# Seven block products in place of eight in two of the six gate/up groups of each feed-forward layer

## The chip, the cores and the metric

The program runs on one core of one Trainium2 chip. The metric is device microseconds of one execution of the whole program. The profile adds the time line of each engine: PE is the matrix engine TensorE (PEld its weight load), DVE is VectorE, ACT is ScalarE, POOL is GpSimd, SP is SyncE, which here issues nearly all transfers.

## The reference

The kernel computes a trunk of four pre-norm layers on one sequence of 256 tokens with 1024 features, all in float32. Each layer adds a token mixer (layers 0 and 3 a sparse attention with compressed, selected and windowed keys, "NSA"; layer 1 a block-sparse attention, "MoBA"; layer 2 a short gated convolution) and then a gated feed-forward network, the "FFN". A last normalisation follows.

```python
D_FF = -(-8 * D_MODEL // (3 * 256)) * 256          # 2816

def swiglu(a, w_gate, w_up, w_down):
    return (jax.nn.silu(a @ w_gate) * (a @ w_up)) @ w_down
...
        h = h + m                                   # m: the mixer's output
        a = rms_norm(h, norm_ffn[i])
        h = h + swiglu(a, ffn_w_gate[i], ffn_w_up[i], ffn_w_down[i])
    return rms_norm(h, norm_final)
```

The change is in `a @ w_gate` and `a @ w_up`: 256 tokens by 1024 features, times two matrices of 1024 by 2816.

## The kernel before

**Operands in two halves.** The matrix engine reads float32 in the type fp32r. Each operand is therefore split in two tiles, a rounded one ("hi", in code `whi`) and what is left ("lo", `wlo` = operand − hi), and a product is three matmuls: hi·hi, hi·lo, lo·hi. For weights the hi copy is made by ScalarE (L119) and the subtraction by VectorE (L123).

**The weight stream.** All weights lie in DRAM as one stream of blocks of 128 × 128, in the order of use. Eight blocks are a *part*: 128 × 1024 elements, 512 KB. `take` hands out the next blocks. When a part is first taken, the parts up to `AHEAD` = 5 (itself included) are loaded and split (`load_part`, `split_part`); there are 4 raw buffers and `W_BUFS` = 5 buffers each of hi and lo. So the two splitting engines may run about four parts ahead of the matrix engine and no further.

**An FFN layer.** `ffn` first computes the gate and up products in groups of up to four column tiles of 128: g = 0, 4, 8, 12, 16 have four, the last, g = 20, has two. In a group of four, two halves of the tokens times gate and up give four accumulators of 128 tokens × 512 columns in PSUM (one bank each; a layer has banks of three tags, A with 4, B with 3, C with 1). Each of the 8 feature tiles k takes 8 blocks, one part: 4 of gate, 4 of up. The matmuls have 128 tokens of the activations as their stationary operand and 512 weight columns as the moving one. A part is 12 matmuls (2 token halves × gate/up × 3), a group of four is 96:

```python
w = [self.take(4) for _ in outs[0]]
for t in range(NT):
    s = slice(t * P, (t + 1) * P)
    for o, (hi, lo) in zip(outs[t], w):
        mm(o, a[:, 0, s], hi, start=(k == 0), stop=False)
        mm(o, a[:, 0, s], lo, start=False, stop=False)
        mm(o, a[:, 1, s], hi, start=False, stop=(k == KT - 1))
```

**Closing a group.** `hidden` applies, for each token half, silu(rstd · gate) on ScalarE (L304), the product with rstd · up on VectorE (L305) and a transposition in 32 × 32 squares on VectorE (L306). The squares are put in place by 16 transfers of SP (`move`, L316, tiles `pt`), four for each part that follows. Two parts after the last of them, `split` makes the hi and lo tiles `ff` of the result (four copies on ScalarE at L202, four subtractions on VectorE at L203). `take` runs these jobs when the stream reaches their part. The down projection (`out_proj`, or `finish` in the last layer) needs `ff` later.

**The norm.** `rstd` = (mean of squares)^−½ of each token is not known when group 0 starts: products are made with the unscaled activations and scaled at the closing. `square` collects the sum of squares `ssq` (ScalarE and GpSimd), the matrix engine sums it over features (`rms_sums`, during the last tile of group 0), and `rms_tokens` computes `rstd` with VectorE (`var`) and GpSimd (L244).

**Order.** The instructions of an engine run in the order in which a scheduler of the framework puts them (by its estimate of what is ready), not as written. Banks and buffers are handed on in the order of their release.

Of the kernel before, what the change touches and what calls it, by code (L numbers as in the profile page):

```python
# [16 lines left out]
P = 128  # L17
# [42 lines left out]
class Kernel:  # L60
    def __init__(self, ctx, tc, ap):
        self.tc, self.nc, self.ap = tc, tc.nc, ap
        self.operands = ctx.enter_context(tc.tile_pool(name="operands", bufs=2))
        self.const = ctx.enter_context(tc.tile_pool(name="const", bufs=1))
        self.wp = ctx.enter_context(tc.tile_pool(name="wp", bufs=3))
        self.work = ctx.enter_context(tc.tile_pool(name="work", bufs=2))
        self.ps = ctx.enter_context(tc.tile_pool(name="ps", bufs=2, space=PSUM))
        self.pos = 0
        self.raw = {}
        self.parts = {}  # L70
        self.jobs = []
        self.nblk = ap["w"].shape[0]
        self.names = [step for step, name, _, c in stream()
                      for _ in range(len(c) // P * (FT if name == "ffn_w_down" else 4 if step == "F" else KT))][::PART]
        self.n = 0

    def uid(self, s):
# [23 lines left out]
    def split_part(self, q):  # L101
        nc = self.nc
        if self.names[q] == "F":
            t = self.operands.tile([P, PART * P], F32, tag="whi", name=f"wf{q}", bufs=W_BUFS)
            nc.sync.dma_start(t, self.ap["w"][q])
            self.parts[q] = (t, t)
            return
        if q not in self.raw:
            self.load_part(q)
        src = self.raw.pop(q)  # L110
        hi = self.operands.tile([P, PART * P], F32R, tag="whi", name=f"whi{q}", bufs=W_BUFS)
        lo = self.operands.tile([P, PART * P], F32R, tag="wlo", name=f"wlo{q}", bufs=W_BUFS)
        lo_eng, hi_eng = (e.get(self.names[q], d) for e, d in ((LO, "v"), (HI, "a")))
        eng = {"p": nc.gpsimd, "v": nc.vector}[lo_eng[q % len(lo_eng)] if q >= 4 else "v"]
        copy = {"a": nc.scalar.copy, "v": nc.vector.tensor_copy}[hi_eng[q % len(hi_eng)] if q >= 4 else "a"]
        n = PART * P // (2 if q < 4 else 1)
        for o in range(0, PART * P, n):
            c = slice(o, o + n)
            copy(hi[:, c], src[:, c])  # L119
            m = n // (PIECES if eng is nc.gpsimd else 1)  # L120
            for b in range(o, o + n, m):
                d = slice(b, b + m)
                eng.tensor_tensor(out=lo[:, d], in0=src[:, d], in1=hi[:, d].bitcast(F32), op=OP.subtract)  # L123
        self.parts[q] = (hi, lo)

    def take(self, n=1):

        q, o = divmod(self.pos, PART)
        assert o + n <= PART
        for x in range(q, min(q + AHEAD, self.nblk)):  # L130
# [156 lines left out]
    def ffn(self, norm):  # L287
# [4 lines left out]
        hs = []  # L292
        q = P // 4
        self.moved = 0

        def hidden(banks, n):

# [3 lines left out]
            for t, (pg, pu) in enumerate(banks):  # L301
                r = self.rstd[:, t:t + 1]
                sg, hf = (self.sb([P, n * P], "pr", bufs=PR_BUFS) for _ in range(2))
                nc.scalar.activation(sg, pg, AF.Silu, scale=r)  # L304
                nc.vector.scalar_tensor_tensor(hf, pu, r, sg, op0=OP.mult, op1=OP.mult)  # L305
                nc.vector.transpose(turned[:, t], hf)  # L306
            rows = self.sb([P, NT, 4, n * q], "pt", bufs=PT_BUFS)
            dst, ds = [self.ff([P, 2, S]) for _ in range(n)], []
            hs.extend(dst)
# [15 lines left out]
            part = max(self.pos // PART + 3, self.moved)  # L325
            for i in range(0, 16, MOVES):
                self.jobs.append((part, move(i)))
                part += 1
            self.moved = part
            self.jobs.append((part + 2, split))  # L330

        for g in range(0, FT, 4):
            n = min(4, FT - g)
            if n == 4:
                banks = [[self.bank(c) for c in row] for row in (("AA", "AA") if g % 8 else ("BB", "BC"))]
                outs = banks
            else:
                outs = [[self.bank("B")] for _ in range(NT)]
                banks = [(o[:, :S], o[:, S:]) for o, in outs]
# [10 lines left out]
            if self.rstd is None:  # L350
                self.rms_tokens()
            hidden(banks, n)
        (self.out_proj if norm < 7 else self.finish)(hs, norm + 1)


    def finish(self, hs, norm):
        nc = self.nc
# [102 lines left out]
    def put_keys(self, dst, p):  # L460
# [3 lines left out]
        for i in range(2):  # L464
            r = slice(i * DH, (i + 1) * DH)
            nc.scalar.copy(dst[r, 0, i, :], f[r])
            nc.vector.tensor_tensor(out=dst[r, 1, i, :], in0=f[r], in1=dst[r, 0, i, :].bitcast(F32), op=OP.subtract)

    def pad_keys(self):
# [79 lines left out]
    def nsa(self, j, norm):  # L549
        nc, at = self.nc, self.begin(norm)  # L550
        mm = nc.tensor.matmul
        w2 = self.sb([P, 2, 2, P], "w2", bufs=1)
        nc.sync.dma_start(w2, self.ap["w2"][j])
        pos = self.sb([P, 2, 16], "pos", bufs=1)
# [326 lines left out]
    def run(self):  # L881
# [39 lines left out]
        self.keys = [const.tile([P, 2, 2, S], F32R, tag=f"keys{i}", name=f"keys{i}") for i in range(4)]  # L921
# [16 lines left out]

def wide_tiles(w, cols):
# [5 lines left out]
def stream():  # L945
# [4 lines left out]
    for i in LAYERS:  # L950
# [36 lines left out]
def tiles(x):  # L987
# [56 lines left out]
```

## Time and profile before

| | |
|---|---|
| time of the kernel, median of 3 runs | 1249.42 us (1249.18 to 1249.9) |
| the profiled execution, its span | 1247.6 us |
| what the median is above the span | 1.8 us |
| busy: PE / PEld | 1225.3 / 1061.5 us |
| busy: DVE / ACT / POOL | 875.0 / 675.6 / 227.3 us |
| the four FFN layers start at | 158.8, 456.7, 729.2, 1059 us |

The span is what the profiler saw between the first and the last instruction; the run's time is counted on the device and has a little around it. "Busy" is the union of an engine's instructions; PE's instructions overlap (a matmul is listed with about 0.39 us while one starts each 0.23 us), so its share tells that work was always queued, not that it was at its fastest. Everything from 20 to 158 us is the mixer of layer 0; the others lie between the FFN layers, at 340 to 457, 638 to 729 and 910 to 1059 us.

### The profile page before, as it was taken

The numbers are of one execution on the slowest core, as the hardware profiler recorded it, in microseconds if no ns is written. First come the engines' busy times: TensorE is split into PE (matmuls) and PEld (weight loads), VectorE is DVE, ScalarE is ACT, GpSimd is POOL, SyncE is SP. The second block draws the span as 40 slices with busy tenths as digits, with TensorE's granted clock in tenths as the row PEclk, the third lists the DMA queues.
The fourth block names the chain that finished last, engine by engine and source line by source line (L and its number), as shares of the span: only waits on it lengthen the run. The fifth ranks groups of instructions, "written<-read, shape, count | busy, mean of one in ns | idle before, by whom it ended". The sixth has DMA issues, their size and how long they took to land.

```text
span 1247.6 us, 19344 instructions
## 1 busy us (share of the span) xinstructions
PE 1225.3 (98%) x6788; PEld 1061.5 (85%) x6788; DVE 875.0 (70%) x1653; ACT 675.6 (54%) x1218; POOL 227.3 (18%) x357
## 2 busy tenths in 40 slices
PE   8999999999999999999999999999999999999997
PEld 8987888888899888888888888888899878888886
DVE  7778785665778795656769886565747797756553
ACT  5588754544456544545444545454446896555443
POOL 1067600000111520000113210000220676000000
PEclk9998999999999999999999999999999999999999
DMA  8741166767555347666665666776666312676772
GB/s 288 247 126 49 52 220 198 239 198 231 188 170 153 102 140 209 216 212 208 220 196 167 195 201 195 212 236 195 208 204 210 118 38 71 208 228 213 226 224 72
DMA packets 91585, 227.20 MB, mean 182 GB/s; under 512 B 17504, under 2 KB 38368, under 8 KB 91488
## 3 DMA queue, kind: packets, MB, share of 16 engines
q1 hardware_dynamic: 91056, 225.41, 57.6%
q8 instruction: 53, 0.87, 0.3%
q10 hardware_dynamic: 432, 0.56, 0.1%
q14 instruction: 44, 0.36, 0.1%
HBM read 213.33 MB, written 1.05 MB: 172 GB/s over the span
## 4 chain that ended last, share of the span: by engine, by line
PE 87%; DVE 5%; ACT 4%; POOL 2%; issue 1%; DMA 1%; POOLq 0%; ACTq 0%; DVEq 0%
PE psA L163 13%; PE psA L167 7%; PE psB L347 6%; PE psB L349 6%; PE psB L348 6%; PE psA L348 5%; PE psA L349 5%; PE psA L347 5%; PE psA L143 2%; PE psB L640 2%; PE psA L144 2%; PE psA L145 2%; PE psB L163 2%; DVE wlo L123 2%; PE psC L349 2%; PE psC L347 2%
## 5 line engine op out<-in xcount | busy, mean ns | idle before, releaser
L123 DVE TENSOR_TENSOR wlo<-raw,whi 128x1024 fp32r<-128x1024 f32 (+1 forms) x366 | 441.0, 1215 | 261.7 <-ACT whi L119 213.7
L119 ACT CAST whi<-raw 128x1024 fp32r<-128x1024 f32 (+1 forms) x379 | 393.2, 1039 | 425.9 <-PE psC L349 91.3
L163 PE MATMUL psA<-ff,whi 128*128 128x512 f32 x686 | 181.5, 393 | 0.1
L163 PEld LDWEIGHTS psA<-ff,whi 128*128 128x128 f32 x686 | 124.6, 189 | 22.7 <-DVE row L847 0.6
L347 PE MATMUL psB<-whi,at 128*128 128x512 f32 x352 | 137.6, 391 | 0.2 <-ACT pr L304 0.2
L349 PE MATMUL psB<-whi,at 128*128 128x512 f32 x352 | 137.2, 390 | 0.0
L348 PE MATMUL psB<-wlo,at 128*128 128x512 f32 x352 | 137.1, 389 | 0.0
L230 POOL TENSOR_TENSOR ssq<-ssq,row 128x256 f32<-128x256 f32 x42 | 33.6, 799 | 393.0 <-ACT row L228 392.2
L143 PE MATMUL psA<-at,whi 128*128 128x256 f32 x352 | 101.3, 288 | 2.0 <-DVE row L411 2.0
L167 PE MATMUL psA<-ff,wlo 128*128 128x256 f32 x686 | 101.5, 283 | 0.0
L167 PEld LDWEIGHTS psA<-ff,wlo 128*128 128x128 f32 x686 | 96.2, 191 | 5.3
L145 PE MATMUL psA<-at,wlo 128*128 128x256 f32 x352 | 99.9, 284 | 0.0
L144 PE MATMUL psA<-at,whi 128*128 128x256 f32 x352 | 99.9, 284 | 0.0
L349 PE MATMUL psA<-whi,at 128*128 128x512 f32 x256 | 99.7, 389 | 0.0
L347 PE MATMUL psA<-whi,at 128*128 128x512 f32 x256 | 99.7, 389 | 0.0
L348 PE MATMUL psA<-wlo,at 128*128 128x512 f32 x256 | 99.7, 389 | 0.0
L448 POOL TENSOR_SCALAR pr<-pr,rc,gates 128x256 f32<-128x256 f32 (+1 forms) x128 | 73.7, 590 | 112.6 <-DVE rc L446 111.3
L347 PEld LDWEIGHTS psB<-whi,at 128*128 128x128 f32 x352 | 66.1, 188 | 14.0 <-ACT pr L304 0.6
L349 PEld LDWEIGHTS psB<-whi,at 128*128 128x128 f32 x352 | 66.1, 188 | 13.8
L348 PEld LDWEIGHTS psB<-wlo,at 128*128 128x128 f32 x352 | 66.1, 188 | 13.6
L123 POOL TENSOR_TENSOR wlo<-raw,whi 128x256 fp32r<-128x256 f32 x96 | 69.6, 763 | 36.7 <-ACT whi L119 16.6
L444 ACT ACTIVATE pr<-pr,mn 128x128 f32<-128x128 f32 (+1 forms) x160 | 71.2, 448 | 5.7 <-DVE mn L441 5.0
(239 smaller groups left out, 2256.1 us busy)
## 6 DMA issues: line engine op xcount, KB each, us to landing
raw<-in_w SPq DMA_DIRECT2D x384, 512.0 KB, 4.3
pt<-pt SPq DMA_DIRECT2D x320, 32.0 KB, 3.1
wf<-in_w SPq DMA_DIRECT2D x16, 512.0 KB, 4.5
h<-in_xt SPq DMA_DIRECT2D x4, 256.0 KB, 4.5
raw<-in_w SPq DMA_DIRECT2D x4, 256.0 KB, 4.8
pt<-pt SPq DMA_DIRECT2D x64, 16.0 KB, 2.9
w<-in_w SPq DMA_DIRECT2D x2, 256.0 KB, 3.9
pt<-in_gfin SPq DMA_DIRECT2D x1, 512.0 KB, 3.9
```

Source lines behind the costliest of these rows:

```text
L119: copy(hi[:, c], src[:, c])
L123: eng.tensor_tensor(out=lo[:, d], in0=src[:, d], in1=hi[:, d].bitcast(F32), op=OP.subtract)
L143: mm(out, wt[0], act[0], start=first, stop=False)
L144: mm(out, wt[0], act[1], start=False, stop=False)
L145: mm(out, wt[1], act[0], start=False, stop=last)
L163: mm(outs[o], w[0], acts[k].rearrange("p i s -> p (i s)"), start=(k == 0), stop=(k == n - 1))
L167: mm(outs[o][:, :S], w[1], acts[k][:, 0, :], start=False, stop=False)
L347: mm(o, a[:, 0, s], hi, start=(k == 0), stop=False)
L348: mm(o, a[:, 0, s], lo, start=False, stop=False)
L349: mm(o, a[:, 1, s], hi, start=False, stop=(k == KT - 1))
L444: nc.scalar.activation(pr[:, c], pr[:, c], AF.Exp, bias=mn[:, j:j + 1], scale=-1.0, accum_out=den[:, j:j + 1])
L448: getattr(nc, PR[j % len(PR)]).tensor_scalar(pr[:, c], pr[:, c], rc[:, j:j + 1], gates[j], op0=OP.mult, op1=OP.mult)
```

## The change

In groups g = 8 and g = 16 of each FFN layer, the first four feature tiles (k = 0 to 3) are computed as a 2 × 2 block matrix product with seven block products in place of eight (Strassen's scheme in Winograd's form). The blocks of the left matrix are (token half) × (k 0–1 or k 2–3), those of the right matrix are (k 0–1 or k 2–3) × (gate or up): B11 is gate and B12 up of k 0–1, B21 gate and B22 up of k 2–3, each 8 blocks in size, one part. Sums of the right blocks are made by VectorE in place: T1 = B12 − B11, T3 = B22 − B12, T2 = B22 − T1, T4 = B21 − T2. A *product* takes one such part, hi and lo, for 6 matmuls of 128 × 512 (2 feature tiles × 3). The tiles k = 4 to 7 stay as they were, 12 matmuls a part. Sums of the left blocks are made once in a layer by GpSimd (`token_sums`).

```diff
-W_BUFS = 5
+W_BUFS = 6
-FF_BUFS = 24
+FF_BUFS = 26
+FAST = ("B11", "T1", "B21", "T2", "B22", "T4", "T3")
+FAST_GROUPS = (8, 16)
+FFN_BANKS = ("BB BA", "AA AB", "BBAA", "AA BB", "BAAB", "B A")
+KX_BUFS = 4
...
+    def fast_part(self, x):
+        q, what = self.seq[x]
+        if what == "B11":
+            self.blocks = {}
+            for i, n in enumerate(("B11", "B12", "B22", "B21")):
+                t = self.blocks[n] = self.block(n)
+                self.load = self.nc.sync.dma_start(t, self.ap["w"][q + i])
+        b = self.blocks
+        hi = self.operands.tile([P, PART * P], F32R, tag="whi", name=f"shi{x}", bufs=W_BUFS)
+        lo = self.operands.tile([P, PART * P], F32R, tag="wlo", name=f"slo{x}", bufs=W_BUFS)
+        self.nc.scalar.copy(hi, b[what])
+        self.nc.vector.tensor_tensor(out=lo, in0=b[what], in1=hi.bitcast(F32), op=OP.subtract)
+        self.parts[x] = (hi, lo)
+        if what == "B11":
+            b["T1"] = self.combine(b["B11"], b["B12"], b["B11"])
+            b["T3"] = self.combine(b["B12"], b["B22"], b["B12"])
+        elif what == "T1":
+            b["T2"] = self.combine(b["T1"], b["B22"], b["T1"])
+        elif what == "B21":
+            b["T4"] = self.combine(b["B21"], b["B21"], b["T2"])
...
+        ahead = AHEAD + (self.names[self.seq[q][0]] in ("ffn", "fast"))
-        while self.jobs and self.jobs[0][0] <= q:
+        while self.jobs and self.jobs[0][0] <= self.when[q]:
...
+            up1, up0, gate0, gate1 = (self.bank(c) for c in tags)
+            product(up1, tokens(0, 0), True)
+            p1 = self.sb([P, 512], "gu")
+            copy(p1, up1, 0)
+            product(up0, summed(0), True)
+            p5 = self.sb([P, 512], "ph", bufs=1)
+            copy(p5, up0, 1)
+            product(gate0, tokens(2, 0), True)
+            product(up1, summed(1), False)
+            u2 = self.sb([P, 512], "pr", bufs=PR_BUFS)
+            copy(u2, up1, 0)
+            product(up0, summed(3), False)
+            product(gate1, tokens(2, 1), True)
+            product(up1, summed(2), False)
+            u3 = self.sb([P, 512], "pr", bufs=PR_BUFS)
+            copy(u3, up1, 1)
...
+            for t, (pg, eg), (pu, eu) in ((0, (gate0, p1), (up0, u2)), (1, (gate1, u3), (up1, p5))):
+                nc.vector.scalar_tensor_tensor(eg, pg, r[t], eg, op0=OP.mult, op1=OP.add)
+                nc.scalar.activation(eg, eg, AF.Silu)
+                nc.vector.scalar_tensor_tensor(eu, pu, r[t], eu, op0=OP.mult, op1=OP.add)
+                nc.vector.tensor_tensor(out=eu, in0=eu, in1=eg, op=OP.mult)
+                nc.vector.transpose(turned[:, t], eu)
...
+    def token_sums(self, norm):
+        x = self.sb([P, 4, S], "ptc", bufs=1)
+        for k in range(4):
+            nc.gpsimd.tensor_scalar(x[:, k, :], self.h[k], self.gain[:, norm, k:k + 1], 1.0, op0=OP.mult, op1=OP.mult)
+        ...                                  # four sums on GpSimd
+        for f in raw:
+            nc.scalar.copy(d[:, 0], f)
+            nc.gpsimd.tensor_tensor(out=d[:, 1], in0=f, in1=d[:, 0].bitcast(F32), op=OP.subtract)
```

The copies p1, p5, u2, u3 are taken by ScalarE out of an accumulator while it goes on being used: the next product into that bank waits for the copy. Besides, the jobs that follow a group are placed by matrix time (`when`: 2 for a part of 12 matmuls, 1 for a product), not by part; the four accumulators use banks of tags A and B alone; the blocks B are loaded into four buffers `kx`, which the attention layers use for their keys (allocated and padded anew for each); the host lays the blocks of the fast groups in the order in which they are loaded.

How this moves the instructions is shown at three places. The first is VectorE around the start of group 16 in layer 1. Before (`wlo169` to `wlo172` are low parts of weight parts 169 to 172; `ff` are low parts of an earlier group's result; L305 and L306 close group 12):

```order
L123 TENSOR_TENSOR wlo169_5881<-raw169_5878,whi169_5880 128x1024
L203 TENSOR_TENSOR ff_627_5742<-pt_626_5741,ff_627_5742 128x256
L203 TENSOR_TENSOR ff_628_5743<-pt_626_5741,ff_628_5743 128x256
L203 TENSOR_TENSOR ff_629_5744<-pt_626_5741,ff_629_5744 128x256
L203 TENSOR_TENSOR ff_630_5745<-pt_626_5741,ff_630_5745 128x256
L123 TENSOR_TENSOR wlo170_5903<-raw170_5900,whi170_5902 128x1024
L305 SCALAR_TENSOR_TENSOR pr_637_5920<-psA_632_5747,rstd_592_5360,pr_636_5919 128x512
L305 SCALAR_TENSOR_TENSOR pr_639_5925<-psA_634_5749,rstd_592_5360,pr_638_5924 128x512
L306 STREAM_TRANSPOSE pt_635_5918<-pr_637_5920 128x512
L306 STREAM_TRANSPOSE pt_635_5918<-pr_639_5925 128x512
L123 TENSOR_TENSOR wlo171_5941<-raw171_5938,whi171_5940 128x1024
```

After (`slo178` to `slo182` are the low parts of the products 3 to 7 of group 16; L120 are the sums T2 and T4, made in place in the buffers of B11 and B21; `wlo171` is the part of k = 4):

```order
L135 TENSOR_TENSOR slo178_5978<-B21_676_5932,shi178_5977 128x1024
L120 TENSOR_TENSOR B11_673_5926<-B22_675_5930,B11_673_5926 128x1024
L258 TENSOR_TENSOR ff_665_5856<-pt_664_5855,ff_665_5856 128x256
L120 TENSOR_TENSOR B21_676_5932<-B21_676_5932,B11_673_5926 128x1024
L135 TENSOR_TENSOR slo179_5999<-B11_673_5926,shi179_5998 128x1024
L135 TENSOR_TENSOR slo180_6019<-B22_675_5930,shi180_6018 128x1024
L361 SCALAR_TENSOR_TENSOR pr_679_6036<-psA_670_5861,rstd_626_5456,pr_678_6035 128x512
L361 SCALAR_TENSOR_TENSOR pr_681_6041<-psB_672_5863,rstd_626_5456,pr_680_6040 128x512
L362 STREAM_TRANSPOSE pt_677_6034<-pr_679_6036 128x512
L362 STREAM_TRANSPOSE pt_677_6034<-pr_681_6041 128x512
L135 TENSOR_TENSOR slo181_6055<-B21_676_5932,shi181_6054 128x1024
L135 TENSOR_TENSOR slo182_6067<-B12_674_5928,shi182_6066 128x1024
```

Two sums stand among the low parts, and the two last low parts of the products stand behind the closing of group 12 (three of the four `ff` rows have moved behind these).

The second place is ScalarE in the same stretch. Before (`whi170` to `whi172` are hi copies, L304 the silus of group 12):

```order
L202 CAST ff_630_5745<-pt_626_5741 128x256
L119 CAST whi170_5902<-raw170_5900 128x1024
L304 ACTIVATE pr_636_5919<-psA_631_5746,rstd_592_5360 128x512
L304 ACTIVATE pr_638_5924<-psA_633_5748,rstd_592_5360 128x512
L119 CAST whi171_5940<-raw171_5938 128x1024
L119 CAST whi172_5958<-raw172_5956 128x1024
```

After (`shi` are hi copies of products; the two L412 are the copies p1 and p5 out of the accumulators of products 1 and 2):

```order
L257 CAST ff_668_5859<-pt_664_5855 128x256
L134 CAST shi179_5998<-B11_673_5926 128x1024
L134 CAST shi180_6018<-B22_675_5930 128x1024
L360 ACTIVATE pr_678_6035<-psA_669_5860,rstd_626_5456 128x512
L360 ACTIVATE pr_680_6040<-psB_671_5862,rstd_626_5456 128x512
L134 CAST shi181_6054<-B21_676_5932 128x1024
L412 ACTIVATE gu_691_6064<-psB_687_6050,rstd_626_5456 128x512
L134 CAST shi182_6066<-B12_674_5928 128x1024
L412 ACTIVATE ph_692_6076<-psA_688_6051,rstd_626_5456 128x512
L167 CAST whi171_6080<-raw171_6078 128x1024
```

The copy p1 stands behind two hi copies, the two silus and a third hi copy.

The third place is GpSimd at the start of layer 1's FFN. Before, the sums of `ssq` stand directly ahead of the power that makes `rstd` (L244); these are the last four of six:

```order
L230 TENSOR_TENSOR ssq_567_5063<-ssq_567_5063,row_573_5080 128x256
L230 TENSOR_TENSOR ssq_567_5063<-ssq_567_5063,row_576_5111 128x256
L230 TENSOR_TENSOR ssq_567_5063<-ssq_567_5063,row_579_5142 128x256
L230 TENSOR_TENSOR ssq_567_5063<-ssq_567_5063,row_582_5173 128x256
L244 TENSOR_TENSOR rstd_592_5360<-var_591_5358,mhalf_104 128x2
```

After (L484 are the four sums, L489 their low parts, L299 is the power):

```order
L285 TENSOR_TENSOR ssq_592_5128<-ssq_592_5128,row_607_5238 128x256
L484 TENSOR_TENSOR row_612_5277<-ptc_611_5272 128x256
L484 TENSOR_TENSOR row_613_5278<-row_612_5277,ptc_611_5272 128x256
L484 TENSOR_TENSOR row_614_5279<-ptc_611_5272 128x256
L484 TENSOR_TENSOR row_615_5280<-ptc_611_5272,row_613_5278 128x256
L489 TENSOR_TENSOR ff_616_5285<-row_612_5277,ff_616_5285 128x256
L489 TENSOR_TENSOR ff_617_5288<-row_613_5278,ff_617_5288 128x256
L489 TENSOR_TENSOR ff_618_5291<-row_614_5279,ff_618_5291 128x256
L489 TENSOR_TENSOR ff_619_5294<-row_615_5280,ff_619_5294 128x256
L299 TENSOR_TENSOR rstd_626_5456<-var_625_5454,mhalf_104 128x2
```

The eight operations on two inputs of the token sums now stand between the last sum of `ssq` and the power.

More of the change, by code (lines that the diff above doesn't have):

```diff
@@ L74, in __init__ @@
                       for _ in range(len(c) // P * (FT if name == "ffn_w_down" else 4 if step == "F" else KT))][::PART]
+        self.seq, q = [], 0
+        while q < self.nblk:
+            if self.names[q] == "fast":
+                self.seq += [(q, w) for w in FAST] + [(q + x, None) for x in range(4, KT)]
+                q += KT
+            else:
+                self.seq.append((q, None))
+                q += 1
+        self.when = [0]
+        for _, what in self.seq:
+            self.when.append(self.when[-1] + (1 if what else 2))
         self.n = 0
@@ L294, in ffn @@
         self.moved = 0
+        sums = self.token_sums(norm)
         def hidden(banks, n):
@@ L323, in split @@
                     self.split(h2.rearrange("p i (a j) -> p i a j", j=q), r3[:, :, c * q:(c + 1) * q])
-            part = max(self.pos // PART + 3, self.moved)
+            at = max(self.when[self.pos // PART] + 2 * after, self.moved)
             for i in range(0, 16, MOVES):
[L327 to L332, printed above, removed]
-            n = min(4, FT - g)
[L334 to L339, printed above, removed]
+                self.later(at, move(i))
+                at += 2
@@ new lines, in spread, with fast, product, tokens @@
+            self.moved = at
+            self.later(at + 4, split)
+        def fast(tags):
+            r = [self.rstd[:, t:t + 1] for t in range(NT)]
+            def product(bank, act, first):
+                hi, lo = self.take(PART)
+                for i in range(2):
+                    c = slice(i * 512, (i + 1) * 512)
+                    ah, al = act(i)
+                    mm(bank, ah, hi[:, c], start=first and i == 0, stop=False, skip_group_check=True)
+                    mm(bank, ah, lo[:, c], start=False, stop=False, skip_group_check=True)
+                    mm(bank, al, hi[:, c], start=False, stop=i == 1, skip_group_check=True)
+            def tokens(k, t):
+                return lambda i: [at[k + i][:, part, t * P:(t + 1) * P] for part in range(2)]
+            def summed(j):
+                return lambda i: [sums[j][:, part, i * P:(i + 1) * P] for part in range(2)]
+            def copy(dst, src, t):
+                nc.scalar.activation(dst, src, AF.Identity, scale=r[t])
+            up1, up0, gate0, gate1 = (self.bank(c) for c in tags)
[14 more added lines that the diff above has]
+            copy(u3, up1, 1)
+            for k in range(4, KT):
+                w = [self.take(4) for _ in range(2)]
+                for t, row in enumerate(((gate0, up0), (gate1, up1))):
+                    s = slice(t * P, (t + 1) * P)
+                    for o, (hi, lo) in zip(row, w):
+                        mm(o, at[k][:, 0, s], hi, start=False, stop=False, skip_group_check=True)
+                        mm(o, at[k][:, 0, s], lo, start=False, stop=False, skip_group_check=True)
+                        mm(o, at[k][:, 1, s], hi, start=False, stop=(k == KT - 1), skip_group_check=True)
+            turned = self.sb([P, NT, 512], "pt", bufs=PT_BUFS)
+            for t, (pg, eg), (pu, eu) in ((0, (gate0, p1), (up0, u2)), (1, (gate1, u3), (up1, p5))):
[4 more added lines that the diff above has]
+                nc.vector.transpose(turned[:, t], eu)
+            spread(turned, 4, 3)
@@ L340, in ffn @@
+        for g, tags in zip(range(0, FT, 4), FFN_BANKS):
+            n = min(4, FT - g)
+            if g in FAST_GROUPS:
+                fast(tags)
+                continue
+            outs = [[self.bank(c) for c in row] for row in tags.split()]
+            banks = outs if n == 4 else [(o[:, :S], o[:, S:]) for o, in outs]
             for k, a in enumerate(at):
```

59 lines of the change are left out of this document (48 added, 11 removed).

## The prediction

> **What bounds the kernel now.** I read the page first: span, busy times, granted clock, the chain that ended last.
>
> ```profile
> span 1247.6 us, 19344 instructions
> PE 1225.3 (98%) x6788; PEld 1061.5 (85%) x6788; DVE 875.0 (70%) x1653; ACT 675.6 (54%) x1218; POOL 227.3 (18%) x357
> PEclk9998999999999999999999999999999999999999
> PE 87%; DVE 5%; ACT 4%; POOL 2%; issue 1%; DMA 1%; POOLq 0%; ACTq 0%; DVEq 0%
> ```
>
> The matrix engine is busy for 98% of the span and holds 87% of the chain. Since that share only says that work was queued, I read it by stage next (window, us; busy time of each engine; granted clock; DMA share; GB/s).
>
> ```profile
> 158.80:180.63 21.83, 21.83 (x99) 18.10 (x98) 17.70 (x26) 11.20 (x14) 2.93 (x4) 1.00 0.72 243
> 202.85:224.62 21.77, 21.77 (x98) 18.03 (x97) 13.99 (x18) 10.98 (x15) 0.00 (x0) 1.00 0.74 230
> 158.80:310.00 151.20, 151.20 (x711) 126.99 (x710) 97.09 (x122) 74.18 (x95) 2.93 (x4) 1.00 0.70 219
> ```
>
> The third row is the whole FFN of layer 0: PE is busy in 151.20 of 151.20 us at full clock. There every matmul taken away is time, so long as the engines that feed PE stay ahead. The second row is group 8, in which VectorE has 7.8 us to spare and ScalarE 10.8. Its first matmul and the first of the next group, in PE's timeline (start, duration), give the price:
>
> ```profile
> 202.85 0.39 PE L347 MATMUL psB<-whi,at 128*128 128x512 f32 x1
> 224.62 0.39 PE L347 MATMUL psA<-whi,at 128*128 128x512 f32 x1
> ```
>
> 96 matmuls lie between these starts: 21.77 / 96 = 0.2268 us each (the 0.39 is the length in the pipeline). A part of 12 is 2.72 us, a product of 6 is 1.36.
>
> **The gain.** A fast group has 7 × 6 + 4 × 12 = 90 matmuls instead of 96; two groups in four layers save 8 × 6 = 48, times 0.2268 = **10.9 us**. Shapes and operand types stay the same, so I take the same pitch.
>
> **VectorE in the fast groups.** Each has three low parts and four sums more. The rows (groups with their mean in ns, then single stretches):
>
> ```profile
> L123 DVE TENSOR_TENSOR wlo<-raw,whi 128x1024 fp32r<-128x1024 f32 x358 | 435.9, 1227 | 261.7 <-ACT whi L119 213.7 <-DMA pt<-pt 19.8 <-PE psB L167 13.5
> L305 DVE SCALAR_TENSOR_TENSOR pr<-psA,rstd,pr 128x512 f32<-128x512 f32 x16 | 11.2, 744 | 0.0
> L306 DVE STREAM_TRANSPOSE pt<-pr 128x512 f32<-128x512 f32 x40 | 26.3, 690 | 0.2
> 166.82 4.62 DVE L123 TENSOR_TENSOR wlo<-raw,whi 128x1024 fp32r<-128x1024 f32 x4
> 200.47 1.43 DVE L203 TENSOR_TENSOR ff<-pt,ff 128x256 fp32r<-128x256 f32 x4
> ```
>
> Back to back a low part takes 4.62 / 4 = 1.155. A sum has the same shape with two inputs, so 1.155 too. In a fast group VectorE has 15 × 1.155, the closing of the plain group before it (2 × 0.744 + 2 × 0.690 = 2.87) and a row split (1.43): 21.6 us, in a window of 90 × 0.2268 = 20.4. That is 1.2 over. In the plain group behind it are 8 × 1.155, the longer closing (6 × 0.744 + 2 × 0.690 = 5.84) and 1.43: 16.5 of 21.8. The pair fits (38.1 of 42.2); the 1.2 must come from the lead. Six buffers allow five parts of lead, up to 13.6 us, and the 5.3 spare us of the plain group fill it. So I price the quantity at nothing; without that cover it would be 1.2 a group, 9.6 in all.
>
> The order matters as much. I replayed the start of group 16, the tighter one, from its first matmul (t = 0), in the order shown above. VectorE comes to the low part of T4 when the closing of group 12 is through and is done with it at 5.8. Product 6 needs it at 5 × 1.36 + 0.23 = 7.0 (its second matmul). T3 is ready at 6.95, needed at 8.4; k = 4 at 8.1, needed at 9.75. Slack 1.2 to 1.65: cost 0.
>
> **ScalarE: the copies out of accumulators.** Product 4 goes into the bank of product 1 and waits for p1; product 5 waits for p5, product 7 for u2. These copies have the shape of the silu. ScalarE's rows:
>
> ```profile
> L119 ACT CAST whi<-raw 128x1024 fp32r<-128x1024 f32 x371 | 388.5, 1048 | 424.7 <-PE psC L349 91.3 <-DMA raw<-in_w 83.1 <-PE psA L349 66.6
> L304 ACT ACTIVATE pr<-psB,rstd 128x512 f32<-128x512 f32 x24 | 16.1, 684 | 2.2 <-PE psB L349 1.7 <-POOL rstd L244 0.3
> 198.24 1.05 ACT L119 CAST whi<-raw 128x1024 fp32r<-128x1024 f32 x1 [2.04 <-DMA raw<-in_w]
> 199.20 1.32 ACT L202 CAST ff<-pt 128x256 fp32r<-128x256 f32 x4
> 205.96 2.52 SPq L316 DMA_DIRECT2D pt<-pt  x4
> pt<-pt SPq DMA_DIRECT2D x320, 32.0 KB, 3.1
> raw<-in_w SPq DMA_DIRECT2D x384, 512.0 KB, 4.3
> ```
>
> A hi copy costs 199.20 − 198.24 = 0.96 in a row of work, a copy 0.684. In the first fast group ScalarE has only the silus before p1: ready at 2.55, needed at 3 × 1.36 = 4.08, cost 0. In group 16 the row split of group 8 stands ahead. Group 8's closing ends 6.0 to 6.6 us after group 12 starts; its 16 transfers take 16 × 0.63 (2.52 / 4) = 10.1 of issue and 3.1 to land, so the rows are there at 19.2 to 19.8 of 21.77, 2.5 to 1.9 before t = 0. ScalarE, which runs in order, then has the row copies (1.32), the hi copies of T2 and B22 (1.92), two silus (1.37), the hi copy of T4 (0.96) and p1 (0.684): 6.25 us, so p1 at 3.75 to 4.35 against 4.08. After another hi copy p5 comes at 5.25 (needed 5.44) and u2 at 7.8 (8.16). Between 0.35 early and 0.3 late I take the late end, rounded: 0.25 × 4 layers = **1.0 us given back**. The bounds are 0, and 1.0 in each of the eight fast groups if the rows land about a microsecond later (the wait then also holds the queue of ScalarE, hence the next hi copies): 8.0.
>
> SP issues the four block loads earlier than the raw parts and moves that stand behind them; a raw part lands after 4.3, and group 12's first part, issued some 5.8 us into group 8, is needed at its end, 20.4. Cost 0, and covered by 10 us.
>
> **Banks.** Without the bank C every group takes one bank that the group before has just closed, at its tenth matmul. For a plain group that is the silu t0 (between groups 0 and 4), or the first step of a fast closing, done 2.4 us ahead. In the first case the power for rstd is on the way, and GpSimd now does eight two-input operations ahead of it:
>
> ```profile
> 164.88 0.74 POOL L230 TENSOR_TENSOR ssq<-ssq,row 128x256 f32<-128x256 f32 x1 [4.07 <-ACT row L228]
> 178.66 0.72 POOL L244 TENSOR_TENSOR rstd<-var,mhalf 128x2 f32<-128x2 f32 x1 [13.04 <-DVE var L242]
> 180.56 0.69 ACT L304 ACTIVATE pr<-psB,rstd 128x512 f32<-128x512 f32 x1
> 183.13 0.39 PE L347 MATMUL psA<-whi,at 128*128 128x512 f32 x1
> 676.69 1.22 DVE L123 TENSOR_TENSOR wlo<-raw,whi 128x1024 fp32r<-128x1024 f32 x1
> 676.92 1.60 POOL L862 TENSOR_TENSOR row<-row,rb 128x256 f32<-128x256 f32 x1 [3.94 <-DVE row L861]
> ```
>
> GpSimd is idle for 13.04 us before the power. One operation takes 0.74 alone and 1.60 beside a low part of VectorE. At the worst each waits for a whole low part: 165.6 + 8 × (0.74 + 1.15) = 180.7, power at 181.4, silu done at 182.1. The bank is wanted by the tenth matmul of group 4, at 183.13. Cost 0, with 1.0 us left; the four extra ScalarE copies go into its idle time.
>
> **Other edits.** Where PE never waits in the FFN, a sixth buffer by itself gives 0 there. The mixers keep five parts ahead, yet have the sixth buffer; see the second rival. The attention's keys lie in the block buffers, so the first block loads after a mixer wait for the last reads of keys, and group 8 is 42 us later: 0. I have no row for the smaller DMA scratch; I take 0.
>
> **Sum.** 1247.6 − 10.9 + 1.0 = 1237.7 for the span; the median of the runs is 1.8 us above it, so **1239.5 us**.
>
> **The rivals.**
>
> 1. *VectorE and ScalarE lose their lead.* If the lead is not rebuilt, the 1.2 us over in each fast group come back: 1239.5 − 1.0 + 9.6 = 1248.1; with part of it 1243 to 1249.5. For it: the pair's budget is 90% full, and p1 sits at its limit. Against: 5 us of spare time in each plain group. Chance 0.17.
>
> 2. *The mixers gain from the sixth buffer.* PE's idle time is 22.3 us, of which 6.4 at the end and 5.9 at the start:
>
> ```profile
> 1180.00:1247.60 67.60, 61.20 (x277) 50.56 (x274) 28.48 (x33) 24.89 (x35) 1.10 (x2) 0.98 0.49 157
> PE psA L191 <- ACT whi L119: 5.9, 1, 5.9
> PE psB L786 <- POOL pr L448: 2.1, 4, 0.8
> 112.00:116.00 4.00, 2.15 (x11) 1.31 (x11) 3.45 (x23) 3.95 (x17) 3.84 (x8) 0.95 0.33 123
> 116.00:122.00 6.00, 5.99 (x18) 4.51 (x19) 4.15 (x14) 3.81 (x13) 5.95 (x11) 0.50 0.01 1
> 1015.00:1019.00 4.00, 2.45 (x13) 1.29 (x11) 3.58 (x20) 3.95 (x17) 2.85 (x6) 1.00 0.44 131
> ```
>
> That leaves 10.0 for the mixers, and the clock in layer 0's attention falls to 0.50 for about 6.4 us with its edges, which costs 3.2. If earlier hi copies smooth that place, 1236.3 or below. Against: the longest waits there are for softmax on GpSimd, which stays. Chance 0.12.
>
> 3. *Slower: the clock falls after the new stalls.* The place is the fast group. PE stalls for 1.2 us there, as in the first rival, at the short waits for copies, and the clock drops as it did at 116 us: 3.2 us a drop. With 9.6 of stalls on top of 1238.5 one needs two drops to pass 1249.42 by more than 0.2%; four give 1238.5 + 9.6 + 12.8 = 1260.9. For it: PE was busy for 2.15 of 4 us before the drop, and no single wait there was over 0.8. Against: 2.45 of 4 us in layer 3 left the clock at 1.00, and a fast group would be over 90% busy. Chance 0.08.
>
> [...]
>
> That the matmuls saved would give nothing is excluded by 151.20 of 151.20.
>
> **How the numbers follow.** Main case, 1235.3 to 1242, 0.60; second rival 0.12; first rival 0.17, of which 0.10 below 1246.9 and 0.07 within 0.2%; third 0.08; the remaining 0.03 is scheduling that I have not seen (0.01 same, 0.02 slower). A measurement of this kernel tells about 0.2% from no change, 1246.9 to 1251.9. Faster 0.60 + 0.12 + 0.10 = 0.82, same 0.08, slower 0.10. The range goes from 1235.0 (nothing given back and the clock kept, 1235.3) to 1246.5 (1.0 given back in all eight groups, 1238.5 + 8.0); about 2 in 10 lie outside.
>
> **What would show it.** Starts of fast groups 20.4 us from the next group's; FFN of layer 0 about 148.7 us instead of 151.2; PE idle in the FFN of about 0.25 us a layer, named with the copies out of the accumulators (L412, p1) in group 16, and none named with `slo` or `psB`; clock 1.00 throughout the FFN; power for rstd done before 181.4. I am wrong if PE waits for low parts in the fast groups, if the clock falls there, or if the mixers take another time than before.

## The result, and the profile after

The changed kernel takes 1256.35 us (median of 4 runs, 1253.26 to 1258.91) beside 1249.3 us of the kernel before: ratio 1.0056, 95% interval 1.004 to 1.0071. It is slower by 0.56%; I had forecast 1239.5 us, faster by 0.8%. The profiled execution is the run of 1258.91 us. The first lines of its page, and the longest waits of the matrix engine but that at the start (us in total, times, longest):

```profile
span 1257.1 us, 19456 instructions
PE 1222.2 (97%) x6740; PEld 1055.8 (84%) x6740; DVE 972.3 (77%) x1741; ACT 718.0 (57%) x1290; POOL 296.5 (24%) x405
PE 48%; DVE 9%; ACT 3%; issue 3%; POOL 2%; DMA 2%; SPq 1%; POOLq 0%; ACTq 0%; DVEq 0%
PE psB L435 <- ACT pr L412: 7.2, 3, 2.7
PE psB L661 <- POOL pr L585: 2.9, 2, 1.4
PE psB L659 <- POOL pr L585: 2.4, 2, 1.3
```

The 48 matmuls are gone (6788 to 6740), but VectorE is busy 97 us more, GpSimd 69, and PE's share of the chain falls from 87 to 48%. Two waits are new or grown. L435 is the first matmul of a part in a fast group, and it waits for a copy out of an accumulator (L412). L659 and L661 are transpositions in layer 1's attention, which wait for the softmax's scaling on GpSimd; the same two had 0.7 us each before:

```profile
PE psB L520 <- POOL pr L448: 0.7, 2, 0.5
PE psB L518 <- POOL pr L448: 0.7, 1, 0.7
```

From the starts of the matmuls I cut both executions into stages and took the difference, in us (layer 0's first stage begins with the span):

| | layer 0 | 1 | 2 | 3 |
|---|---|---|---|---|
| down projection of the layer ahead, and the mixer | −0.83 | +6.16 | +0.05 | +0.91 |
| group 4 | +0.18 | 0 | 0 | +0.96 |
| group 8 (fast) | −1.36 | −1.36 | −1.36 | −1.36 |
| group 16 (fast) | +2.75 | −1.73 | +2.89 | +3.72 |

Groups 0, 12 and 20 are unchanged (but −0.12 in layer 1's group 20); all of it adds up to the +9.5 of the span. Group 8 gained what 6 matmuls cost (6 × 0.2268 = 1.36) everywhere, group 16 only in layer 1; the 0.37 that it gains there beyond that is time that the kernel before had lost, whose group 16 took 22.12 in this layer and 21.76 in the others. The windows of group 8 in layer 0 and of group 16 in layers 0 and 1:

```profile
202.21:222.61 20.40, 20.40 (x92) 16.90 (x90) 15.12 (x18) 11.80 (x15) 0.00 (x0) 1.00 0.78 229
244.37:268.88 24.51, 22.34 (x91) 17.99 (x90) 17.82 (x21) 14.90 (x19) 4.17 (x8) 0.93 0.61 189
549.82:570.21 20.39, 20.39 (x91) 16.89 (x90) 16.33 (x20) 12.85 (x16) 0.00 (x0) 1.00 0.83 275
```

In the second row PE stands still for 2.2 us, and the granted clock is 0.93 in place of 1.00. The timelines of ScalarE at the end of the products tell the two layers apart, layer 0 (first three rows) and layer 1 (last three), with SP and VectorE in layer 0 between them:

```profile
251.46 2.00 ACT L167 CAST whi<-raw 128x1024 fp32r<-128x1024 f32 x2
256.58 1.04 ACT L167 CAST whi<-raw 128x1024 fp32r<-128x1024 f32 x1 [3.12 <-DMA raw<-in_w]
257.53 0.68 ACT L412 ACTIVATE pr<-psB,rstd 128x512 f32<-128x512 f32 x1
240.42 12.20 SPq L113 DMA_DIRECT2D raw<-in_w  x5
251.04 1.22 DVE L171 TENSOR_TENSOR wlo<-raw,whi 128x1024 fp32r<-128x1024 f32 x1
556.08 2.00 ACT L167 CAST whi<-raw 128x1024 fp32r<-128x1024 f32 x2
559.53 0.69 ACT L412 ACTIVATE pr<-psB,rstd 128x512 f32<-128x512 f32 x1 [1.45 <-PE psB L403]
563.16 1.05 ACT L167 CAST whi<-raw 128x1024 fp32r<-128x1024 f32 x1 [2.94 <-DMA raw<-in_w]
```

The copy is u3, the fourth. In layer 0 a hi copy stands ahead of it, that of the *next* group's first part, which is not needed for another 8 us. It waits 3.12 us for its transfer. SP could not issue that transfer, the last of five raw loads, before VectorE's low part at 251.04 gave a raw buffer free; it lands at 256.6. Meanwhile product 7 had been done, and PE's timeline shows what u3 held up:

```profile
255.70 0.39 PE L437 MATMUL psB<-whi,at 128*128 128x512 f32 x1
258.26 0.50 PE L435 MATMUL psB<-whi,at 128*128 128x512 f32 x1 [2.17 <-ACT pr L412]
```

In layer 1 u3 stands ahead of that hi copy, which then waits as long without harm. Layers 2 and 3 have layer 0's order, with waits of 2.4 and 2.7.

### The profile page after: what moved, and what is told of

Its sections match the earlier page's. It is cut to its first block, busy times and chain, and to the rows that moved or that the text cites. A ratio compares the mean times of both kernels' runs of the same rounds, so it can differ in the third digit from the quotient of the medians.

```text
span 1257.1 us, 19456 instructions
## 1 busy us (share of the span) xinstructions
PE 1222.2 (97%) x6740; PEld 1055.8 (84%) x6740; DVE 972.3 (77%) x1741; ACT 718.0 (57%) x1290; POOL 296.5 (24%) x405
## 4 chain that ended last, share of the span: by engine, by line
PE 48%; DVE 9%; ACT 3%; issue 3%; POOL 2%; DMA 2%; SPq 1%; POOLq 0%; ACTq 0%; DVEq 0%
PE psA L218 8%; PE psA L222 4%; DVE wlo L171 3%; PE psB L461 2%; PE psB L463 2%; PE psB L462 2%; PE psA L461 2%; PE psA L463 2%; PE psA L462 2%; SPq L376 1%; PE psB L218 1%; DMA raw<-in_w 1%; ACT whi L167 1%; PE psB L782 1%; PE psA L198 1%
## 5 line engine op out<-in xcount | busy, mean ns | idle before, releaser
L171 DVE TENSOR_TENSOR wlo<-raw,whi 128x1024 fp32r<-128x1024 f32 (+1 forms) x334 | 411.3, 1249 | 139.8 <-ACT whi L167 134.2
L167 ACT CAST whi<-raw 128x1024 fp32r<-128x1024 f32 (+1 forms) x347 | 357.1, 1039 | 283.7 <-DMA raw<-in_w 188.0
L200 PE MATMUL psA<-at,wlo 128*128 128x256 f32 x352 | 100.6, 286 | 0.0
L461 PE MATMUL psB<-whi,at 128*128 128x512 f32 x224 | 87.9, 392 | 0.6 <-ACT pr L360 0.6
L463 PE MATMUL psB<-whi,at 128*128 128x512 f32 x224 | 87.3, 390 | 0.0
L461 PE MATMUL psA<-whi,at 128*128 128x512 f32 x224 | 87.3, 390 | 0.0
L463 PE MATMUL psA<-whi,at 128*128 128x512 f32 x224 | 87.3, 390 | 0.0
L462 PE MATMUL psB<-wlo,at 128*128 128x512 f32 x224 | 87.2, 390 | 0.0
L462 PE MATMUL psA<-wlo,at 128*128 128x512 f32 x224 | 87.2, 389 | 0.0
L171 POOL TENSOR_TENSOR wlo<-raw,whi 128x256 fp32r<-128x256 f32 x96 | 74.7, 812 | 38.2 <-ACT whi L167 17.2
L134 ACT CAST shi<-B 128x1024 fp32r<-128x1024 f32 x56 | 57.8, 1049 | 37.3 <-DVE B L120 25.3
L135 DVE TENSOR_TENSOR slo<-B,shi 128x1024 fp32r<-128x1024 f32 x56 | 66.8, 1217 | 8.1 <-ACT shi L134 8.1
L198 PEld LDWEIGHTS psA<-at,whi 128*128 128x128 f32 x352 | 68.1, 193 | 2.7 <-DVE row L548 2.5
```

Of the source, the lines that this page charges most:

```text
L198: mm(out, wt[0], act[0], start=first, stop=False)
L200: mm(out, wt[1], act[0], start=False, stop=last)
```

## The experiments

Each was timed beside the kernel before, with 95% intervals, but for the seventh, which ran once.

**1. u3 ahead of the next group's hi copy.** The first edit leaves that part out while product 7 is taken, the second puts its hi copy behind u3 on ScalarE:

```diff
-        ahead = AHEAD + (self.names[self.seq[q][0]] in ("ffn", "fast"))
+        ahead = AHEAD + (self.names[self.seq[q][0]] in ("ffn", "fast") and self.seq[q][1] != "T3")
...
+                    with self.tc.issue_after(self.hold):
+                        self.split_part(x)
+                    self.hold = None
...
-            copy(u3, up1, 1)
+            self.hold = copy(u3, up1, 1).ins
```

> The changed kernel, with one edge of order more: in a fast group the hi copy of the part after k = 7 (the next group's first part) is issued by ScalarE behind the copy u3, in every layer as it already is in layer 1. In the profile of the changed kernel group 16 takes 24.5, 20.4, 24.7 and 25.5 us in layers 0 to 3, and in the three slow ones that hi copy stands ahead of u3 and waits for its part. Theory 'late copy': only this order makes the waits, and the clock drop that follows each; group 16 then takes 20.4 in all four layers, no wait on a copy out of an accumulator is left, 13.4 us come back: 1243 us (1241 to 1245). Rival 'no lead' (VectorE and ScalarE have too much to do in the fast groups): the wait moves to the next low part or hi copy, group 16 stays at 23 or more in some layers, over 1251 us.

Measured: 1245.67 us (1243.87 to 1246.66), 0.9972 of before (0.9962 to 0.9982). Group 16 takes 20.40 us in all four layers (the windows of layers 0, 2 and 3), and no wait on L412's copies is left:

```profile
245.06:265.46 20.40, 20.40 (x91) 16.89 (x90) 15.94 (x18) 14.12 (x17) 3.51 (x7) 1.00 0.62 202
814.06:834.46 20.40, 20.40 (x92) 16.90 (x91) 15.50 (x16) 13.67 (x17) 0.00 (x0) 1.00 0.63 194
1142.51:1162.91 20.40, 20.40 (x92) 16.90 (x90) 15.38 (x17) 14.32 (x17) 0.00 (x0) 1.00 0.66 207
```

So 'late copy' holds, and VectorE and ScalarE do keep up. By the medians 10.7 us came back, not 13.4, and the time is 0.7 above the range expected. The 13.4 is from the profiled execution of the changed kernel, its slowest run, with five clock drops ahead of the end; from that execution to this one's (span 1242.3 us) it is 14.8.

**2. A fifth raw buffer, the order as it was.** 

```diff
-RAW_BUFS = 4
+RAW_BUFS = 5
-FF_BUFS = 26
+FF_BUFS = 25
```

> The changed kernel with five raw buffers instead of four (and 25 instead of 26 buffers ff, to make room): the order on ScalarE stays, u3 behind the next group's hi copy, but that part can be loaded a low part earlier. Theory 'late copy, and the hi copy waits for a transfer that waits for a raw buffer': the hi copy no longer waits 3 us, group 16 takes 20.4 to 22 us in all layers, 1243 to 1248 us. If the hi copy waits for a hi buffer or for ScalarE's own backlog ('no lead'), nothing changes: 1254 to 1258.

Measured: 1245.3 us (1244.01 to 1246.64), 0.9974 (0.9965 to 0.9984); group 16 at 20.4 to 20.5, and group 4 at 21.76 in all four layers, so the 0.18 and 0.96 us that it had lost came back too. In layer 0's ScalarE timeline the three hi copies ahead of u3 now run without a pause, and u3 waits for PE alone:

```profile
250.63 3.08 ACT L167 CAST whi<-raw 128x1024 fp32r<-128x1024 f32 x3
254.02 0.69 ACT L412 ACTIVATE pr<-psB,rstd 128x512 f32<-128x512 f32 x1 [0.31 <-PE psB L403]
```

The cause has two halves, and taking away either is enough: the order, and the transfer that waits for a raw buffer.

**3. Five operand buffers.** 

```diff
-W_BUFS = 6
+W_BUFS = 5
-        ahead = AHEAD + (self.names[self.seq[q][0]] in ("ffn", "fast"))
+        ahead = AHEAD
```

> The changed kernel with five operand buffers and five parts ahead everywhere, as before the change. Theory for the mixers: the sixth buffer alone moves low parts on GpSimd ahead of the softmax's scaling, on which the matrix engine waits (layer 1's mixer was 6.2 us longer than before the change, a clock drop in it included); with five buffers it is as before. In the fast groups the hi copy in question can then no longer stand ahead of u3, but the lead is a part shorter. Late copy and this theory together: 1237 to 1243 us. If the mixers are slowed by the shared key buffers or by GpSimd's token sums, layer 1's mixer stays 4 to 6 us longer: 1243 to 1247. Rival 'no lead': the fast groups wait for low parts, 1.2 us or more in each: 1247 or more.

Measured: 1248.01 us (1246.45 to 1250.23), 0.9996 (0.9987 to 1.0005). Layer 1's mixer is back (177.97 us, 177.69 before), but the fast groups wait, as the rival 'no lead' has it; group 8 takes 21.87, 21.09, 20.45 and 21.93 us. The run's waits on low parts of products and plain parts and on p1:

```profile
PE psA L402 <- DVE slo L135: 1.3, 2, 0.7
PE psB L462 <- DVE wlo L171: 1.0, 2, 0.5
PE psB L401 <- ACT gu L412: 0.9, 2, 0.6
```

So the sixth buffer, with the part of lead that it allows, is what pays for the 1.2 us by which VectorE is estimated to be over its time in a fast group. It is also what slows layer 1's mixer: there the number of parts ahead was the same.

**4. The kernel before with six buffers.** 

```diff
-W_BUFS = 5
+W_BUFS = 6
-    nc = bacc.Bacc("TRN2", target_bir_lowering=False, num_devices=1)
+    nc = bacc.Bacc("TRN2", target_bir_lowering=False, num_devices=1, dynamic_dma_scratch_size=1024)
```

> The kernel before with six operand buffers in place of five (and the smaller DMA scratch, which makes room), five parts ahead as before, nothing else. Theory for the mixers: layer 1's mixer gets 3 to 6 us longer, as in the changed kernel, with waits of the matrix engine on the softmax's scaling there; the FFN stays as it is: 1252 to 1256 us. If the shared key buffers or the token sums slow the mixers, there is no change: 1249 to 1250. My prediction's second rival (the mixers gain): 1246.

Measured: 1269.51 us (1264.4 to 1271.22), 1.0163 (1.0145 to 1.018), much worse than either theory. The profiled execution is the fastest of the five (1264.4 us), so what follows explains some 15 of the 21 us. Layer 1's mixer takes 4.7 us longer, within the 3 to 6 expected, and layer 0's mixer with the start 2.3; but the FFN does not stay as it is: group 16 loses 5.2 us over the layers, group 20 2.1. The first waits but that at the start:

```profile
PE psB L347 <- ACT pr L304: 4.9, 4, 2.0
PE psB L520 <- POOL pr L448: 2.9, 2, 1.4
PE psB L518 <- POOL pr L448: 2.4, 2, 1.3
```

The last two are those of the changed kernel in layer 1, to a tenth; so the buffer makes them, not the keys or the token sums. (The smaller DMA scratch came with it here; experiment 3 has that scratch with five buffers, and its mixer is as before.) The first is the late copy's pattern again, in a kernel without fast groups. ScalarE's timeline at the start of group 20 in layer 0 has the two silus (L304) of group 16 behind hi copies that waited for transfers:

```profile
266.15 1.05 ACT L119 CAST whi<-raw 128x1024 fp32r<-128x1024 f32 x1 [2.29 <-DMA raw<-in_w]
270.79 1.04 ACT L119 CAST whi<-raw 128x1024 fp32r<-128x1024 f32 x1 [0.21 <-DMA raw<-in_w]
271.74 1.26 ACT L304 ACTIVATE pr<-psB,rstd 128x512 f32<-128x512 f32 x2
```

GpSimd's timeline in layer 1 shows how the buffer makes the other two, in the kernel before (two rows) and the changed kernel (two rows), with a transposition of the latter that waits:

```profile
412.74 2.31 POOL L448 TENSOR_SCALAR pr<-pr,rc 128x128 f32<-128x128 f32 x4 [2.45 <-DVE rc L446]
416.87 3.01 POOL L123 TENSOR_TENSOR wlo<-raw,whi 128x256 fp32r<-128x256 f32 x4 [1.81 <-PE psB L521]
414.55 2.13 POOL L171 TENSOR_TENSOR wlo<-raw,whi 128x256 fp32r<-128x256 f32 x3 [7.67 <-PE psA L200]
416.66 3.28 POOL L585 TENSOR_SCALAR pr<-pr,rc 128x128 f32<-128x128 f32 x4
419.54 0.33 PE L661 MATMUL psB<-ident,pr 128*128 128x128 f32 x1 [1.44 <-POOL pr L585]
```

The low parts wait for PE in both. In the kernel before they wait for L521 and stand behind the scaling. With one more buffer they wait for an earlier matmul, L200 (in this experiment L145), and the scheduler has put them ahead of the scaling. That it does so because they count as ready earlier is my reading of its order; no run shows its reasons.

**5 and 6. One buffer held during attention.** Experiment 1, and an idle tile takes one hi and one lo buffer while an attention mixer runs; experiment 6 adds the fifth raw buffer.

```diff
+        self.held = [self.operands.tile([P, PART * P], F32R, tag=tag, name=self.uid("held"), bufs=W_BUFS)
+                     for tag in ("whi", "wlo")]
+        for t in self.held:
+            self.nc.gpsimd.memset(t[:, :2].bitcast(F32), 0.0)
...
+            if i % 3 < 2:
+                self.hold_buffers()
...
+            if i % 3 < 2:
+                self.give_buffers()
             self.ffn(2 * i + 1)
```

`give_buffers` lets GpSimd read two columns of each held tile, together with the last part of `h`.

> The kernel of the first experiment (u3 first), and while an attention mixer runs one hi and one lo buffer are held by an idle tile, so that the mixer has five and the FFN six; GpSimd then has the low parts of the mixers' output weights behind the same softmax scalings as before the change. Theory 'the sixth buffer moves low parts ahead of the scaling': layer 1's mixer falls from 182.3 to about 177.7 us, its waits on the scaling from 5.3 to 1.4, and with fewer clock drops the run comes to 1241 us (1239.5 to 1242.5). Rival: the key buffers or the token sums slow the mixers through other work on GpSimd: 1245 to 1246, layer 1's mixer above 181.

> The fifth experiment with five raw buffers (and 25 instead of 26 buffers ff): the waits at the start of group 4 in layers 0 and 3 (0.15 and 0.87 us with four raw buffers, none with five) go too. All gate/up groups then take their matmuls' time, 22.3, 21.8, 20.4, 21.8, 20.4, 10.9: 1240 us (1238.5 to 1241.5), which is my predicted sum with nothing given back. If the FFN needs the 26th buffer ff, group 20 or the down projection gets a wait, over 1242.

Measured: 1245.74 us (1244.51 to 1246.66), 0.9973 (0.9964 to 0.9982), and 1246.29 us (1244.59 to 1247.67), 0.9978 (0.9969 to 0.9987). Both miss the times expected. Layer 1's mixer is at 177.7 as expected, but the first matmul of the program waits 10.7 us instead of 5.9: in layer 0 the held tiles are in the way of the start, a fault of my edit. In 5 group 4 lost 2.4 us over the layers, where experiment 1 had lost 1.0. In 6 the waits of group 4 were halved and not gone, and group 12 got one of about 1 us in layers 0 and 3.

**7. The clock by itself.** Into the groups 4, 8, 12 and 16 of the kernel before, one stall each (g = 4 has no long copy, g = 16 three):

```diff
+                if k == 4 and n == 4 and g:
+                    x = self.sb([P, 512], "pr", bufs=PR_BUFS)
+                    last = nc.scalar.copy(x[:, :8], outs[1][1][:, :8])
+                    for _ in range(g // 4 - 1):
+                        last = nc.scalar.copy(x, outs[1][1])
+                    late = self.ff([P, 2, S])
+                    with self.tc.issue_after(last.ins):
+                        nc.scalar.copy(late, a.bitcast(F32))
+                    a = late
...
-                        mm(o, a[:, 1, s], hi, start=False, stop=(k == KT - 1))
+                        mm(o, a[:, 1, s], hi, start=False, stop=(k == KT - 1 or n == 4 and k == 3), skip_group_check=True)
```

(The last line ends the sum after k = 3 for the copy, and the next tile goes on with it.)

> The kernel before with one stall of the matrix engine put into the groups 4, 8, 12 and 16 of each layer, to measure the clock by itself: before the tile k = 4 ScalarE makes a short copy out of the last accumulator, then 0, 1, 2 or 3 copies of 128 x 512, then a copy of the activations that the next matmuls read. The stalls are estimated at 1.2, 1.8, 2.4 and 3.0 us from copies of 0.68 (four of each length, in 22 us of otherwise full work). Theory of my third rival, with the size that the changed kernel shows: the granted clock falls for 3.4 us (1.7 us lost) after the stalls of 2.2 us and more, in most of the eight, and not after 1.2: 33.6 of stalls and 8 x 1.7 = 13.6, 1295 us or so. If the clock falls only after a stretch that is idle throughout, there is no drop: 1282. If any stall does it: 16 drops, 1309.

Measured: 1289.62 us. The ladder came out with two steps and not four: the gaps between matmul starts are 1.5 us in groups 4, 8 and 12 (1.9 at most), and 4.0, 4.0, 4.0 and 3.0 in group 16. None of the twelve short stalls was followed by a drop; of the four long ones two were, and each of these drops lasted 6.8 us. So four stalls and not eight were above 2.2 us, half of them made a drop, and length alone does not decide. In the traces of the kernel before and of the changed kernel the drops begin whole windows of 3.413 us apart: 331.0 in the first, and 47.0, 121.0, 56.0, 42.0 and 25.0 from each to the next in the second. The windows of such a grid at the long stalls of this run's layers 0, 1 and 2, with the window behind each (cut to within 0.1 us of the grid; behind the length stand PE, PEld, DVE, ACT and POOL, then the clock):

```profile
261.45:264.86 3.41, 1.57 (x7) 0.95 (x6) 1.85 (x2) 1.69 (x3) 0.00 (x0) 1.00 0.85 226
264.87:268.28 3.41, 1.62 (x7) 1.35 (x8) 0.56 (x1) 1.69 (x3) 0.00 (x0) 1.00 0.76 206
568.68:572.09 3.41, 1.26 (x6) 0.72 (x4) 1.92 (x2) 2.05 (x4) 0.00 (x0) 1.00 0.74 199
572.10:575.51 3.41, 2.00 (x5) 1.64 (x6) 0.18 (x1) 1.32 (x3) 0.00 (x0) 0.51 0.73 203
852.06:855.47 3.41, 1.11 (x5) 0.57 (x4) 1.92 (x2) 2.20 (x4) 0.00 (x0) 1.00 0.71 206
855.48:858.89 3.41, 2.15 (x5) 1.78 (x6) 0.03 (x1) 1.18 (x3) 0.00 (x0) 0.50 0.74 192
```

In layer 0 a gap of 4.0 us fell on the seam of two windows, with 7 matmuls in each, and the clock stayed at 1.00; in layers 1 and 2 it left 6 and 5 in one window, and the next ran at half clock (0.51 and 0.50), as did the one after it. The gap of 3.0 in layer 3 lies across a seam too.

**8. The held buffer in layer 1 alone**, else experiment 5:

```diff
-            if i % 3 < 2:
+            if i % 3 == 1:
```

> The fifth experiment with the idle tiles held in layer 1's mixer alone. There they brought the mixer back to 177.7 us, but in layer 0 they made the first matmul wait 4.8 us longer, at the start of the program. So: layer 0's mixer 158 to 159 us as in the first experiment, layer 1's 177.7, the gate/up groups 22.3, 21.8 to 22.7, 20.4, 21.8, 20.4, 10.9: the first experiment's 1245.67 minus 4.6, 1241 us (1239.5 to 1242.5). If the gain in layer 1 is lost again elsewhere (a clock drop in another place), 1243 to 1245.

Measured: **1239.03 us** (1238.05 to 1240.07), 0.9922 of before (0.9908 to 0.9936), the fastest of all. The page, and its waits on the scaling in layer 1:

```profile
span 1237.3 us, 19452 instructions
PE 85%; DVE 7%; ACT 3%; POOL 2%; issue 2%; DMA 1%; POOLq 0%; ACTq 0%; DVEq 0%
PE psB L679 <- POOL pr L591: 0.7, 2, 0.5
PE psB L677 <- POOL pr L591: 0.7, 1, 0.7
```

Layer 1's mixer takes 177.73 us, the groups 8 and 16 save 10.7 of the 10.9 us, and PE's share of the chain is back at 85%.

## Why the prediction was wrong, point by point

The sum with nothing given back is a span of 1236.7 us. The 1257.1 of the profiled execution is 20.4 more: 13.4 in group 16 of layers 0, 2 and 3, 6.2 in layer 1's mixer, 1.1 at group 4, and −0.4 from the other stages together.

- **The gain** was right: 0.2268 us a matmul, 1.36 a fast group.
- **VectorE in the fast groups** was right as priced, at nothing: it runs on its lead, which needs the sixth buffer (experiment 3). In experiment 1 it is busy for 36.9 us of group 8 and group 12 of layer 0, where I had 38.1.
- **ScalarE's copies: the step that failed.** I replayed p1, p5 and u2 in the order of layer 1 and left out u3, and took one layer's order for all four. p1, p5 and u2 made no wait anywhere, so the 1.0 us that I gave back for them was nothing; in layer 1's group 16, p1 was through 2.4 us after the start and not 3.75 to 4.35. u3, behind the next group's hi copy in layers 0, 2 and 3, made 7.2 us of waits, and the drops that followed 3 × 1.7. That is 12.3 of the 13.4 us by which these three groups miss 20.4; the remaining 1.1 is not resolved. My upper bound for this term was 1.0 a group; it measured 4.1 to 5.1.
- **SP at cost 0** was the same slip: I asked whether the late part was in time for PE, not whether a hi copy that waits for it blocks something else on ScalarE.
- **Six buffers at 0, or a gain in the mixers** (second rival): wrong in sign. Layer 1's mixer lost 6.2 us: 3.9 of waits on the scaling (5.3 against 1.4), 1.7 of a clock drop, the rest not resolved. Experiments 3, 5 and 8, with five buffers in that mixer, have it back at 177.7 to 178.0 us.
- **The slow rival** had the mechanism that came, the clock falling after new stalls, but with a wrong stall and price. A drop is one window of 3.41 us at half clock, 1.7 us, or two such, as the 6.8 us before the change. Three followed u3's waits, in the window behind (first row the window of the wait, then the next; clock 1.00, then 0.51):

```profile
256.18:259.59 3.41, 1.33 (x6) 1.11 (x7) 1.72 (x2) 2.00 (x3) 0.00 (x0) 1.00 0.87 295
259.60:263.01 3.41, 3.41 (x10) 2.67 (x9) 2.16 (x2) 1.72 (x2) 0.00 (x0) 0.51 0.81 220
```

  Here the window was not idle: six matmuls ran in it. The twelve short stalls of experiment 7 (1.5 us, 1.9 at most) made no drop.
- **The bank at group 4.** GpSimd's sums were inside my bound. They ended 11 us after the last sum of `ssq`, not 15.1, and the power still came late in layer 3, at 1089.8 for a matmul that cost 0.96 us in all. What I missed stands in VectorE's and GpSimd's timelines there: `var` queues behind a low part that waits for its hi copy, and the power takes 1.65 instead of 0.72 beside the next low part. That hi copy had itself waited 1.13 us for its transfer, and with a fifth raw buffer (experiment 2) group 4 waits nowhere: it looks like the fault of u3 in another queue, though experiment 6, with the same buffer, still lost 0.5 us there in layers 0 and 3.

```profile
1086.73 1.23 DVE L171 TENSOR_TENSOR wlo<-raw,whi 128x1024 fp32r<-128x1024 f32 x1 [0.95 <-ACT whi L167]
1087.88 0.16 DVE L297 TENSOR_SCALAR var<-psA 128x2 f32<-128x2 f32 x1
1088.11 1.65 POOL L299 TENSOR_TENSOR rstd<-var,mhalf 128x2 f32<-128x2 f32 x1 [5.42 <-DVE var L297]
```

The predicted time itself, 1239.5, is that of experiment 8, where the two orders are mended; this shows the sum of the gain, not that the prediction was right for the kernel as it was changed. That the two lie within half a microsecond is in part luck: there group 4 loses 1.1 us that I had at nothing, and layer 0's mixer, with one window at half clock in place of two, gains 0.9 that I had not counted.

What stays open in part is the spread of the runs (1253.26 to 1258.91). The granted clock on record is 0.996 in the fastest and 0.992 in the other three. A difference of 0.004 is 5.0 us, about three windows at half clock, and the fastest is 2.9 to 5.7 us ahead; so the clock can account for most of it, as far as these rounded figures tell. Which stalls made no drop in the faster runs cannot be seen, since only the slowest run has a trace.

## What to carry to other kernels

Here a deeper ring of buffers did not only give lead: with it the scheduler put work that is not urgent earlier into a queue that runs in order, where it waited for a transfer (the hi copy in layer 0's group 16, 3.12 us) with urgent small work behind it (u3, for which PE stood still for 2.17 us). When a change adds small copies that the matrix engine waits for, list in every layer what stands ahead of each in its queue, and what that in turn waits for. Then hold the non-urgent work behind the copy, or take its wait away (1245.67 and 1245.3 us here, instead of 1256.35).

## What was not expected of the hardware

For each window of the 3.413 us grid at full clock (experiment 7), in the traces of the kernel before and of the changed kernel, I estimated the share of time in which no matmul was being started. It is worked out from the start times: a matmul of 128x512 is taken as 0.227 us, one of 128x256 as 0.12 and a narrower one as 0.11, the usual distances of their starts in these traces; the start and the end of the program are left out. In the windows ahead of the three drops behind u3's waits the share is 63, 73 and 83%, with 6, 5 and 4 matmuls of 128x512 in them. Ahead of the drops in the mixers of layers 1 and 3 of the changed kernel it is 85 and 65%, ahead of the one in layer 0's mixer before the change 68%. The highest share in these two traces with no drop behind it is 57%, in layer 3's mixer before the change. So few windows show no threshold, nor that this share alone decides.

In these rows VectorE, too, is slowed while GpSimd does the same kind of work, as GpSimd is beside VectorE. While GpSimd made the four low parts of the token sums (1.69 us each, beside 0.74 for a sum alone), four low parts of VectorE took 1.70 each instead of 1.155:

```profile
1075.93 6.76 POOL L489 TENSOR_TENSOR ff<-row,ff 128x256 fp32r<-128x256 f32 x4
1076.97 6.80 DVE L171 TENSOR_TENSOR wlo<-raw,whi 128x1024 fp32r<-128x1024 f32 x4
```
